# Projection halves of a hybrid block written in program order, slot by slot, with two-block attention units, unscaled queries and first values as plain products

## The chip, the cores and the metric

The kernel runs on one core of a Trainium2 chip. The metric is the device time of one execution in microseconds (us). A core has a matrix engine (PE in the profile, with its weight loads as PEld), a vector engine (DVE), a scalar engine (ACT), a general engine (POOL), and a sync engine (SP) that here only issues transfers. Each engine works through its own list of instructions in order and waits at an instruction until what it needs is there.

## The reference

One layer, one sequence of 2048 tokens, width 1024, all in float32. Cut to what matters:

```python
mod = silu(c) @ w_ada + b_ada;  shift, scale, gate = split(mod, 3)
h = rms_norm(x, norm_w) * (1 + scale) + shift
a, b, g_conv, q, k, v, g_attn, m_conv, m_attn = split(h @ w_in)     # one projection to 10240 columns
u = silu(layer_norm(depthwise_causal_conv(a * sigmoid(b)))) * silu(g_conv)   # 31 taps
y_conv = u @ w_conv_out
q, k = rope(rms_norm(q)), rope(rms_norm(k))                          # 12 heads of 128
# 3 groups of 4 heads, dilation 1, 4, 16: blocks of 128 queries against their own and the previous key block
o = softmax over the groups' log denominators, weighted sum of the 3 groups' outputs
y_attn = (o * silu(g_attn)) @ w_attn_out
y = sigmoid(m_conv) * y_conv + sigmoid(m_attn) * y_attn
x + gate * (y @ w_out)
```

## The kernel before

**The projection.** The tokens are worked in two halves of 1024. In a half the 80 column blocks of 128 are done in pairs, 40 pairs (the code's "quads": two column blocks by two token blocks of 512 by two halves of the depth). A quad is multiplied by a Strassen-Winograd scheme with seven products (`PRODUCTS`) in place of eight. Each operand is split into two float32r parts, a high one (ACT copies, `shB`, `shT`) and a low one (the difference, `slB`, `slT`, on POOL or DVE), and a product is 12 matmuls of 128x512 (hi*hi, hi*lo, lo*hi for four depth chunks). One product is a slot. The quarters of the activations and their sums are A11, A12, A22, S1 to S4; weight quarters B11 to B22 and sums T1 to T4 come from POOL in the first half of the tokens and are stored for the second (`tT_d`).

**Order of quads in a half.** First two value quads in alternating slots, then 16 query, key and value quads (`qkv_quad`; called the chain below), then 22 more: 8 for the convolution's input (`ab_quad`) and 14 gates. `quad` is a generator; a slot runs one product, copies or adds its bank to a scratch tile ("spare_hi", "spare_lo", 8 places of 512 columns) and prepares the weights of a slot four later.

**Rotary step.** `rotate` squares a query or key quad (ACT), sums the squares over the head with PE (`pssq`, `pssk`, L490), brings the sums through memory into columns (`ssq_d`, `stq`), takes the power -1/2 on POOL (L136), and brings the result through memory back as rows (`rsq`, `rsk`, L530). DVE multiplies the rotated quad by them (L534), and it is stored to `qk_d`. Values are turned by PE (`ptv`, L453) and stored.

**Attention** (`attend`) works one block of 128 queries at a time, in steps of one slot each: loads, scores on PE (`ps`, L583) with mask, scale and minimum on DVE (L592) and exponential on ACT (L593); transposes on PE (`ptp`, L598) with a copy on DVE (L600); values on PE (`po`, L620). For the last group `weigh` combines the three groups. The blocks of the last quads are worked beside the first gates of the half. The convolution's taps (`conv_parts`) are DVE instructions, 3.1 of them a slot on the average.

**What sets the order.** PE's list is the program's order (`manual_schedule`). All other lists are set by a scheduler that plans with its own time line, except where `keep` pins an instruction. Stores of the weight sums are issued by ACT, all other transfers by SP.

**After the halves** comes a tail: attention's and the convolution's output projections, and the last projection by the same seven products.

Of the kernel before, what the change touches and what calls it, by code (L numbers as in the profile page):

```python
# [38 lines left out]
WS = 5  # L39
# [18 lines left out]
def tile_hybrid_block(  # L58
# [17 lines left out]
    BANKS = {"z": 2, "s": 1, "t": 2, "o": 3}  # L76
# [7 lines left out]
    tab_d = dram.tile([2, 64, HS], F32, name="tab_d")  # L84
# [15 lines left out]
    t_d = {}  # L100
    keep = tc.keep_in_program_order
# [37 lines left out]
    edge.tile([P, 120], F32, name="edge")  # L139
# [11 lines left out]
    wraw_c = tc.tile_pool(name="wr", bufs=10, side="right", reuse_waits="tile")  # L151
# [4 lines left out]
    pe_order.__enter__()  # L156

    PLACE = {"A11": (0, 0), "A12": (1, 0), "A22": (1, 1), "S1": (0, 1), "S2": (0, 2), "S3": (1, 2), "S4": (0, 3)}
# [20 lines left out]
    rp, at, cv, gpa, xh = {}, {}, {}, {}, {}  # L179
# [11 lines left out]

    def spare_tiles():
        spares[:] = [quarter_tile(1, 3, hl, f"spare_{hl}", F32) for hl in ("hi", "lo")]
# [13 lines left out]

    conv_todo = []
# [4 lines left out]

    def column_steps(half, c0, c1, lo_engines):

        q, got = {}, []
        where = {"B11": (0, c0), "B21": (1, c0), "B12": (0, c1), "B22": (1, c1)}

        def load(name):
            t = q[name] = wr.tile([P, 4, P], F32, tag="wr", name=f"w{name}_{half}_{c0}")  # L220
            src = w_in[where[name][1] // P, where[name][0]] if name in where else t_d[name, c0]
            nc.sync.dma_start(t.rearrange("p k c -> p (k c)"), src)

        def combine(name, dst, x0, x1):
            if dst is None:
                dst = wr.tile([P, 4, P], F32, tag="wr", name=f"w{name}_{c0}")
# [3 lines left out]
        def split(name, eng):  # L230
# [4 lines left out]
            if half == 0 and name not in where:  # L235
                t_d[name, c0] = dram.tile([P, 512], F32, name=f"t{name}_{c0}_d")
                nc.scalar.dma_start(t_d[name, c0], q[name].rearrange("p k c -> p (k c)"))

        def fetch(n):
            if half:  # L240
# [6 lines left out]
        def step(n):  # L247
            if half == 0:
                if n == 2:
                    combine("T1", q["B11"], q["B12"], q["B11"])  # L250
                    combine("T2", None, q["B22"], q["T1"])
                if n == 4:
                    combine("T3", q["B12"], q["B22"], q["B12"])
                if n == 6:
                    combine("T4", q["B21"], q["B21"], q["T2"])
            split(PRODUCTS[n][1], nc.vector if n in lo_engines else nc.gpsimd)

        return got, step, fetch, load

    def quad(name, got, sink, place=None, cut=lambda x: x, side="s"):  # L260
# [4 lines left out]
        def product(n, ps, more=False):  # L265
            ah, al = quarters[PRODUCTS[n][0]]
            wh, wl = got.pop(0)
            terms = [t for k in range(4) for t in ((wh[:, k], ah[:, k]), (wh[:, k], al[:, k]), (wl[:, k], ah[:, k]))]
            for m, (w, x) in enumerate(terms):
                nc.tensor.matmul(ps, w, x, start=(m == 0 and ps.name not in first), stop=(m == 11 and not more),  # L270
                                 skip_group_check=True)
            first.add(ps.name)

        def kept(ps, t, col):
            dst = place(t, col) if place else scratch()
            nc.scalar.activation(dst, cut(ps), AF.Copy)  # L276
            return dst

        product(0, pa, True)
        s1 = kept(pa, 0, 0)  # L280
        yield
        pb = bank(side, f"pb{name}")
        product(1, pb)
        nc.vector.tensor_tensor(s1, s1, cut(pb), op=ALU.add)
        sink(0, 0, s1)
        yield
        product(2, pa, True)
        s2 = kept(pa, 0, 1)
        yield
        pc = bank(side, f"pc{name}")  # L290
        product(3, pc, True)
        s5 = kept(pc, 1, 0)
# [1293 lines left out]
```

## Time and profile before

| | |
|---|---|
| median of 3 runs | 2673.28 us (2673.21 to 2675.82) |
| profiled execution | 2674.34 us, span from first to last instruction 2672.6 us |
| busy share of the span | PE 89%, DVE 69%, ACT 44%, POOL 49% |
| granted PE clock, mean | 0.943 |
| transfers | 462.80 MB, 173 GB/s over the span |

The time lies 1.7 us above the span. A busy PE is not a fast PE: a matmul that runs at half the clock is busy twice as long, so the number of matmuls in a stretch says more than the busy share. In the trace a row's duration of a matmul overlaps the next one's, so starts are compared.

### The profile page before, as it was taken

What the parts mean: (1) busy time and instruction counts of PE and PEld (TensorE: products, weight loads), DVE (VectorE), ACT (ScalarE), POOL (GpSimd) and SP (SyncE); (2) the same over time, 40 slices, a digit from 0 to 9 for tenths busy, and PEclk for the clock granted to TensorE, in tenths of its full rate; (3) what the DMA queues carried; (4) which work ended last, traced back from release to release, by engine and by line L of the source; (5) the groups of instructions that cost most, each with busy time, mean ns of one, the idle gap of its engine ahead of it and who ended that gap; (6) DMA issues with size and microseconds to landing.
All of it is one profiled execution on the core that took longest, in us unless ns stands there. A gap on an engine that the chain in (4) does not pass through costs nothing. (4 is left out here: it accounts for less than half of the span.)

```text
span 2672.6 us, 36779 instructions
## 1 busy us (share of the span) xinstructions
PE 2390.2 (89%) x11580; PEld 1940.7 (73%) x11580; DVE 1842.7 (69%) x3034; ACT 1184.5 (44%) x2313; POOL 1300.8 (49%) x1014
## 2 busy tenths in 40 slices
PE   6766788988888999999888899888999998999999
PEld 5545666777667888877667777776788887788787
DVE  2779655555588999995755444459899985777744
ACT  3544444444745444465444444465344443332221
POOL 3567755575444677876544444333565760000131
PEclk7787889999999999999989999999999999999999
DMA  7266545565545444575455556654554559876553
GB/s 266 78 172 227 149 135 163 155 197 172 173 145 162 148 154 167 182 232 151 135 149 154 162 144 187 197 165 140 165 160 131 159 173 316 255 228 222 184 166 107
DMA packets 349708, 462.80 MB, mean 173 GB/s; under 512 B 43460, under 2 KB 176068, under 8 KB 349384
## 3 DMA queue, kind: packets, MB, share of 16 engines
q1 hardware_dynamic: 312200, 392.77, 49.3%
q10 hardware_dynamic: 37312, 67.67, 6.8%
q8 instruction: 92, 1.51, 0.2%
q14 instruction: 104, 0.85, 0.1%
HBM read 295.14 MB, written 164.63 MB: 172 GB/s over the span
## 5 line engine op out<-in xcount | busy, mean ns | idle before, releaser
L233 POOL TENSOR_TENSOR slB<-wB,shB 128x512 fp32r<-128x512 f32 x196 | 271.8, 1387 | 342.0 <-ACT shB L232 289.5
L233 POOL TENSOR_TENSOR slT<-wT,shT 128x512 fp32r<-128x512 f32 x200 | 278.5, 1393 | 213.5 <-ACT shT L232 186.8
L232 ACT ACTIVATE shB<-wB 128x512 fp32r<-128x512 f32 x240 | 150.6, 628 | 276.2 <-PE paab L270 41.3
L233 POOL TENSOR_TENSOR slT<-wB,shT 128x512 fp32r<-128x512 f32 x120 | 171.7, 1441 | 109.8 <-ACT shT L232 74.2
L232 ACT ACTIVATE shT<-wT 128x512 fp32r<-128x512 f32 x200 | 125.9, 629 | 214.3 <-issue 20.9
L600 DVE COPY pT<-ptp 128x256 f32<-128x256 f32 (+1 forms) x192 | 73.2, 382 | 175.7 <-PE ptp L598 175.0
L352 DVE SCALAR_TENSOR_TENSOR ce<-us,pair_taps,ce 128x512 f32<-128x512 f32 x240 | 180.4, 752 | 5.5
L323 DVE SCALAR_TENSOR_TENSOR ce<-ut,chan,ce 128x512 f32<-128x512 f32 x240 | 178.6, 744 | 0.0
L336 DVE SCALAR_TENSOR_TENSOR cq<-ut,chan,cq 128x512 f32<-128x512 f32 x208 | 155.0, 745 | 0.5
L227 POOL TENSOR_TENSOR wB<-wB,wB 128x512 f32<-128x512 f32 x80 | 112.8, 1410 | 54.8 <-DVE slB L233 49.8
L593 ACT ACTIVATE sm<-sm,osb 128x256 f32<-128x256 f32 (+1 forms) x128 | 59.8, 467 | 168.1 <-DVE osb L592 143.4
L598 PE MATMUL ptp<-ident,sm 128*128 128x128 f32 x332 | 74.5, 295 | 58.8 <-ACT sm L593 57.8
L620 PE MATMUL po<-v,pT 128*128 128x128 f32 x560 | 99.0, 285 | 23.1 <-DVE pT L600 20.7
L232 ACT ACTIVATE shT<-wB 128x512 fp32r<-128x512 f32 x120 | 75.3, 628 | 99.2 <-PE pbab L270 11.1
L592 DVE CUSTOM_DVE_ANT_0 sm<-ps,mask 128x256 f32<-128x256 f32 (+1 forms) x192 | 73.1, 381 | 63.0 <-PE ps L583 38.5
L620 PEld LDWEIGHTS po<-v,pT 128*128 128x128 f32 x560 | 86.3, 197 | 36.4 <-DVE pT L600 24.8
L135 POOL TENSOR_SCALAR stf<-stf 128x4 f32<-128x4 f32 x4 | 1.3, 324 | 199.6 <-DVE stf L1235 199.6
L598 PEld LDWEIGHTS ptp<-ident,sm 128*128 128x128 f32 x332 | 42.6, 148 | 72.9 <-ACT sm L593 70.1
L583 PE MATMUL ps<-qk 128*128 128x128 f32 x384 | 79.7, 292 | 0.7 <-DVE osb L622 0.7
L1407 ACT ACTIVATE yh<-yq 128x512 fp32r<-128x512 f32 x48 | 27.3, 623 | 118.2 <-POOL yq L1401 45.3
L606 POOL COPY stm<-part 128x4 f32<-128x4 f32 x64 | 13.6, 214 | 121.6 <-DMA part<-acc_d 97.9
L296 POOL TENSOR_TENSOR spare_lo<-spare_lo 128x512 f32<-128x512 f32 x41 | 66.5, 1621 | 4.4 <-ACT spare_lo L276 4.4
(789 smaller groups left out, 8175.5 us busy)
## 6 DMA issues: line engine op xcount, KB each, us to landing
wB<-in_w_in_dram SPq DMA_DIRECT2D x280, 256.0 KB
wT<-tT_d SPq DMA_DIRECT2D x160, 256.0 KB
tT_d<-wB ACTq DMA_DIRECT2D x120, 256.0 KB
qk<-qk_d SPq DMA_DIRECT2D x192, 128.0 KB
v_d<-vev SPq DMA_DIRECT2D x48, 256.0 KB
qk_d<-spare_hi SPq DMA_DIRECT2D x48, 256.0 KB
qk_d<-spare_lo SPq DMA_DIRECT2D x48, 256.0 KB
v<-v_d SPq DMA_DIRECT2D x192, 64.0 KB
```

The costliest lines, as they stand in the source:

```text
L227: nc.gpsimd.tensor_tensor(dst, x0, x1, op=ALU.subtract)
L232: nc.scalar.activation(h, q[name], AF.Copy)
L233: eng.tensor_tensor(l, q[name], h.bitcast(F32), op=ALU.subtract)
L296: nc.gpsimd.tensor_tensor(s3, s3, s5, op=ALU.add)
L323: stt(box["e"], e[:, 1 + j : 513 + j], chan[:, cb, 2 * j : 2 * j + 1], box["e"], op0=ALU.mult, op1=ALU.add)
L336: stt(box["o"], o[:, 2 + j : 514 + j], w, psum_o, op0=ALU.mult, op1=ALU.add)
L352: stt(dst, box["both"][:, 1 + j : 513 + j], pair_taps[:, cb, j : j + 1], box["e"], op0=ALU.mult, op1=ALU.subtract if j == 0 else ALU.add)
L583: nc.tensor.matmul(ps[:, P * i : P * i + P], box["q"], kt, start=True, stop=True)
L592: nc.vector.tensor_tensor_reduce(sm[:, :w], ps[:, :w], m[:, 256 - w :], ISQ, 3e38, ALU.add, ALU.min, low)
L598: nc.tensor.transpose(pt[:, P * i : P * i + P], box["sm"][:, P * i : P * i + P], ident)
L600: nc.vector.tensor_copy(pT[:, :w], pt[:, :w])
L620: nc.tensor.matmul(po[:, :P], box["pT"][:, P * i : P * i + P], vt, start=(i == 0), stop=(i == nk - 1))
```

## The change

All five engines' lists are now the program's order during the value, query and key quads of a half, and up to 6 slots after the last of them; outside of it the scheduler orders the other engines as before. A slot runs in a fixed sequence of named places.

```diff
-    LEAD = WS - 1
-        next(running[i], None)
-        prepare(s + LEAD)
-        for f in agenda.pop(s, ()):
-            f()
-        if waiting and (s % 4 != 3 or i % half_jobs >= QJ):
-            main.enter(attend(*waiting.pop(0)))
-        for f in main.turn():
-            f()
+        if waiting and s % 2:
+            for d, where, f in unit(*waiting.pop(0)):
+                at_slot(s + 3 + d, f, where)
+        run_agenda(s, "load")
+        ask(s + AHEAD + 2)
+        for where in ("act", "pe", "vec"):
+            run_agenda(s, where)
+        prepare(s + AHEAD)
+        run_agenda(s, "act2")
+        next(running[i], None)
+        run_agenda(s, "tail")
+        run_agenda(s, "store")
-WS = 5
+WS, WR, AHEAD = 4, 10, 3
+MANUAL, ORDER_END = (True, True), 6
-    BANKS = {"z": 2, "s": 1, "t": 2, "o": 3}
+    BANKS = {"z": 2, "s": 2, "t": 1, "u": 1, "o": 2}
```

Attention goes by units of two blocks (up to 128x512 scores in a bank), a new one every second slot, and each step has its place. Queries are stored unscaled; the root of a query's squares is turned by PE into a column (`queries`, `query_roots`) and multiplies the scores in the instruction that adds the mask. Keys are scaled as before, at fixed slots.

```diff
-            nc.vector.tensor_tensor_reduce(sm[:, :w], ps[:, :w], m[:, 256 - w :], ISQ, 3e38, ALU.add, ALU.min, low)
+            rq = heads_rq[half, u - u % 2]
+            for i, b in enumerate(bs):
+                a, z = cols[i][0], 256 * i + 256
+                nc.vector.tensor_tensor_reduce(sm[:, a:z], ps[:, a:z], m[:, 256 - (z - a) :], rq[:, b, u % 2 : u % 2 + 1], 3e38,
+                                               ALU.add, ALU.min, box["low"][i])
-        return (load, fetch, scores, turn_p, values, *((turn_o,) if g == 0 else ()))
+        return ((-3, "load", load), ((-1, "store", fetch) if half else (-2, "load", fetch)), (0, "pe", scores), (1, "act", exps), (2, "tail", turn_p), (3, "act", weigh),
+                (3, "tail", values), (4, "store", keep), (5, "pe", turn_o), (6, "store", keep_o))
...
-        squares(0)
-        for d, f in ((1, lambda: sums(0)), (1, lambda: squares(1)), (2, lambda: sums(1)), (2, part(0, 0)), (3, roots), (3, part(0, 1)),
-                     (4, part(1, 0)), (5, part(1, 1)), (5, spread), (7, lambda: scaled(0)), (8, lambda: scaled(1))):
-            at_slot(s0 + d, f)
+            sq = ((e4 + 1, 0, 0), (e5, 1, 1), (e5 + 1, 0, 1), (e6 + 1, 1, 0))
+            start, last = e5 + 2, e6 + 3
...
+        at_slot(last, rows, "act2")
+        if which == 0:
+            at_slot(last + 1, queries, "tail")
+            at_slot(last + 2, query_roots)
+        else:
+            at_slot(last, keys, "store")
+            at_slot(last + 1, key_roots)
+            at_slot(last + 2, key_spread, "store")
+            s = last + 3
+            for i in range(2):
+                at_slot(s + i, key_scale(i))
+                at_slot(s + i + 1, store(i), "load")
```

In the chain, the first product of a quad now stands between the fifth and the sixth product of the quad before it. The first two value quads of the first half are plain products, 16 of them (`PLAIN`), that need only A11 and A21 for their first six slots; two low parts in three or more of the seven go to DVE in the first half (`QKV_LO`), and the sums of two banks that POOL added are now added by DVE from the bank. The tanh gates come first in a half, three of them before the convolution's first quad, and the silu gates last. Weight sums are stored by SP a slot after they are made. Rotary tables are stored already permuted for each group and loaded anew when the group changes. Attention in the first half may begin only when the second half's activations are prepared (`later_done`, slot 78).

```diff
+        for i in range(len(chain)):
+            j = len(jobs) + i
+            slots += [(j, n) for n in range(early, 5)] + [(j + 1, 0)] * (i + 1 < len(chain)) + [(j, 5), (j, 6)]
+            early = True
+    PLAIN = ((0, "B11", "A11", "C11"), (1, "B11", "A11", "C11"), (0, "B12", "A11", "C12"), (1, "B12", "A11", "C12"),
+             (0, "B11", "A21", "C21"), (0, "B12", "A21", "C22"),
...
+QKV_LO = (((1, 3, 5), (1, 3, 5), (0, 1, 3, 5, 6)), ((), (), (1, 3, 5)))
+FIRST_GATES, BETWEEN = 3, ((1, 1, 1, 1, 2, 1, 2, 2), (1, 1, 2, 1, 1, 1, 1, 3))
-        gates = [(GC0, g_d, AF.Silu), (MC0, mc_d, AF.Tanh), (MA0, ma_d, AF.Tanh)]
+        todo = [(gate_quad, half, g, cb) for g in ((MC0, mc_d, AF.Tanh), (MA0, ma_d, AF.Tanh), (GC0, g_d, AF.Silu)) for cb in range(0, KC, 2)]
-                nc.scalar.dma_start(t_d[name, c0], q[name].rearrange("p k c -> p (k c)"))
+                at_slot(slot_now[0] + 1, lambda: nc.sync.dma_start(d, t), "store")
```

**ACT, start of the kernel, before.** `xsq` are the squares of the second token block, on which A12, A22 and all sums S wait; `shT` are high parts of weight sums.

```order
L237 DMA tT_6656_d<-wB_0_6656_213 128x512
L237 DMA tT_6912_d<-wB_0_6912_215 128x512
L232 ACTIVATE shT_0_6656_398<-wT_6656_396 128x512
L237 DMA tT_6656_d<-wT_6656_396 128x512
L237 DMA tT_6656_d<-wB_0_6656_365 128x512
L232 ACTIVATE shT_0_6912_421<-wT_6912_419 128x512
L237 DMA tT_6912_d<-wT_6912_419 128x512
L702 ACTIVATE xsq_1_428<-hf_1_172 128x512
```

The same place after:

```order
L289 ACTIVATE shB_p_1_381<-wB_p_222 128x512
L289 ACTIVATE shB_p_2_385<-wB_p_224 128x512
L289 ACTIVATE shB_p_3_400<-wB_p_226 128x512
L289 ACTIVATE shB_p_4_417<-wB_p_220 128x512
L883 ACTIVATE xsq_1_435<-hf_1_179 128x512
```

The squares stood behind high parts of POOL's weight sums; they now stand behind high parts of loaded weights, and no sum is needed there.

**ACT, first gates of the first half, before.** `L402` is a gate's function, `L593` the exponential of a block's scores; a table load stands wherever the function's set changes.

```order
L402 ACT_TABLE_LOAD
L402 ACTIVATE spare_hi<-spare_hi 128x512
L593 ACT_TABLE_LOAD
L593 ACTIVATE sm_0_4_5808,stm_0_4_5807<-sm_0_4_5808,stm_0_4_5807 128x256
L608 ACTIVATE stm_0_4_5807<-stm_0_4_5807 128x3
L403 DMA g_d<-spare_hi 128x512
L232 ACTIVATE shT_0_2304_5889<-wB_0_2304_5597 128x512
L613 ACTIVATE part_0_4_5755<-part_0_4_5755,stm_0_4_5807 128x128
L402 ACT_TABLE_LOAD
```

After, the only load in the gates of this half stands where the silu gates begin, behind the last tanh gate:

```order
L451 ACTIVATE spare_hi<-spare_hi 128x512
L452 DMA ma_d<-spare_hi 128x512 x2
L246 ACTIVATE shT_0_2048_8133<-wB_0_2048_7984 128x512
L327 ACTIVATE spare_lo<-pag_g_d_0_8113 128x512
L246 ACTIVATE shB_0_2048_8167<-wB_0_2048_7986 128x512
L451 ACT_TABLE_LOAD
```

ACT's whole list holds 48 table loads before and 6 after.

**DVE, chain, scaling of a quad, before (a query quad of the first half).** `sm` is the instruction on a block's scores, `pT` the copy of its transposes.

```order
L600 COPY pT_0_2_4325<-ptp_0_2_4323 128x128
L503 SCALAR_TENSOR_TENSOR tmk_4_10_4506<-spare_lo,hw,cos_665 128x512
L504 SCALAR_TENSOR_TENSOR tmk_4_11_4507<-spare_lo,hw,sin_666 128x512
L534 TENSOR_TENSOR spare_hi<-spare_hi,rsq_4_4238 128x1024 x2
L592 ISA sm_0_3_4378,osb_0_3_4377<-ps_0_3_4375,mask_120 128x128
```

After (a key quad of the second half):

```order
L778 ISA sm_1_2_13572,osb_1_2_13571<-ps_1_2_13566,mask_120,rqq_3_12414 128x256
L778 ISA osb_1_2_13571 128x1
L644 TENSOR_TENSOR spare_lo<-spare_lo,rsk_4_13561 128x1024
L512 TENSOR_TENSOR spare_hi<-spare_hi,pcv_4_13453 128x512
L796 COPY pT_1_0_13598<-ptp_1_0_13593 128x512
L644 TENSOR_TENSOR spare_lo<-spare_lo,rsk_4_13561 128x1024
```

The scaling of queries is gone from DVE's list. That of keys stands in two parts, one in each of two slots, with a bank's addition and a unit's copy behind the first.

More of the change, by code (lines that the diff above doesn't have):

```diff
@@ L262, in quad, with step @@
         pa = bank("z", f"pa{name}")
         first = set()
[L265 to L271, printed above, removed]
+        def step(n, ps, more=False):
+            product(PRODUCTS[n][0], ps, got.pop(0), ps.name not in first, not more)
@@ L302, in quad @@
         yield
-        product(6, pa)
-        if place:
-            kept(pa, 1, 0)
+        step(6, pa)
         sink(1, 0, pa, s1)
@@ L445, in qkv_quad, with step, evict @@
-        return quad(n, got, sink, place, cut, side)
-    def turn_v(half, _, u0, g, reg, n):
-        s0 = slot_now[0]
+        cut, place = token_views(g)
+        at = slots_of[half, which, pair]
+        (turn_v if which == 2 else rotate)(half, which, u0, g, reg, n, at)
+        pa = bank("z", f"pa{n}")
+        first = set()
+        def step(m, ps, more=False):
+            product(PRODUCTS[m][0], ps, got.pop(0), ps.name not in first, not more)
+            first.add(ps.name)
+        def evict(dst, ps):
+            nc.scalar.activation(dst, cut(ps), AF.Copy)
@@ L1032, in attention_shut @@
     def attention_shut():
-        assert not waiting and not main.parts
         shut(at)
@@ L1161, in tile_hybrid_block @@
                 load_ai0(n - 3)
[L1162 removed]
+    run_conv(len(conv_todo))
+    assert not agenda, agenda
     shut(gpa)
```

1044 lines of the change are left out of this document (628 added, 416 removed), and 3 rows, old and new, of the table PLAIN.

## Prediction

> **What bounds the kernel now.** I read the page first, then the busy time by stages, then PE's waits in the stages that lose most, and last the rows around single waits. On the page, PE is the busiest engine, and nothing else comes near it:
>
> ```profile
> span 2672.6 us, 36779 instructions
> PE 2390.2 (89%) x11580; PEld 1940.7 (73%) x11580; DVE 1842.7 (69%) x3034; ACT 1184.5 (44%) x2313; POOL 1300.8 (49%) x1014
> ```
>
> The stages: the start with the first two value quads (to 136), the chain of the first half (to 658), its first gates with attention beside them (to 850), gates with the convolution, then the same for the second half (value quads from 1168, chain from 1214, gates from 1709), and the tail from 2213. In each row stand the limits, the length, the busy time and count of each engine, the granted clock and the transfers.
>
> ```profile
> core 0: us, PE busy (x) PEld busy (x) DVE busy (x) ACT busy (x) POOL busy (x), PEclk, DMA share, GB/s
> 0.00:136.00 136.00, 94.04 (x449) 73.49 (x450) 65.85 (x80) 56.88 (x90) 65.86 (x65) 0.79 0.50 175
> 136.00:658.00 522.00, 422.98 (x2203) 336.42 (x2203) 324.36 (x434) 233.71 (x503) 340.21 (x222) 0.89 0.58 170
> 658.00:850.00 192.00, 157.13 (x798) 128.88 (x797) 138.01 (x407) 114.14 (x248) 76.45 (x91) 0.94 0.50 155
> 850.00:1150.00 300.00, 300.00 (x1325) 248.39 (x1324) 281.56 (x402) 135.61 (x234) 232.24 (x185) 1.00 0.50 170
> 1168.00:1214.00 46.00, 39.94 (x169) 32.79 (x169) 30.64 (x40) 25.00 (x37) 28.91 (x21) 0.93 0.71 216
> 1214.00:1709.00 495.00, 436.64 (x2446) 356.40 (x2445) 266.67 (x391) 225.63 (x478) 233.21 (x154) 0.94 0.54 154
> 1709.00:1950.00 241.00, 217.20 (x1072) 179.27 (x1072) 188.05 (x475) 136.75 (x288) 96.15 (x103) 0.96 0.57 171
> 2213.00:2672.00 459.00, 442.51 (x1904) 355.35 (x1902) 292.76 (x449) 128.72 (x215) 50.60 (x40) 0.98 0.66 209
> ```
>
> From 850 to 1150 PE is never idle and has the full clock: 300 us for 1325 matmuls, 0.2264 us each; I take 0.2252, since a few of them are other work. That gives the floor of any stage, if I know how many of its matmuls are products (line 270) and how many are small:
>
> ```profile
> 136.00:658.00 522.00, 364.88 (x1345) 267.49 (x1345) 0.89 0.58 170
> 658.00:850.00 192.00, 117.75 (x446) 86.20 (x447) 0.94 0.50 155
> 1214.00:1709.00 495.00, 351.42 (x1346) 259.35 (x1346) 0.94 0.54 154
> 1709.00:1950.00 241.00, 177.24 (x699) 134.70 (x700) 0.96 0.57 171
> ```
>
> Small ones, and a wait with what it does to the clock, on PE's list (start, duration, matmul, and the idle time before it):
>
> ```profile
> 406.28 0.79 PE L270 MATMUL paq<-S_hi,shT 128*128 128x512 f32 x1 [2.04 <-ACT spare_lo L276]
> 406.87 0.63 PE L270 MATMUL paq<-S_lo,shT 128*128 128x512 f32 x1
> ...
> 409.43 0.51 PE L270 MATMUL paq<-S_lo,shT 128*128 128x512 f32 x1
> ...
> 421.54 0.61 PE L620 MATMUL po<-v,pT 128*128 128x128 f32 x4
> ...
> 422.46 0.47 PE L270 MATMUL paq<-A_hi,shT 128*128 128x512 f32 x1
> 428.62 0.64 PE L490 MATMUL pssq<-sqq,sel 128*32 128x128 f32 x16
> 429.19 0.71 PE L620 MATMUL po<-v,pT 128*128 128x128 f32 x4
> ```
>
> From 421.54 to 422.46 PE ran nine small matmuls, 0.1 us each; the 16 for the sums of squares took 0.57, 0.036 each, and a half has 384 of these. So the floor of the first chain is 1345 x 0.2252 = 303, plus 384 x 0.036 = 14, plus 474 x 0.1 = 47: 364. It takes 522: 158 too much, of which 99 are idle and the rest slow matmuls. In the same way: first gates 446 x 0.2252 + 352 x 0.1 = 136 of 192, 56 too much; second chain 303 + 14 + 72 = 389 of 495, 106 too much (58 idle); its gates 157 + 37 = 195 of 241, 46 too much. The rest of the gates and the tail have little to lose.
>
> Slow matmuls come from waits: after the 2.04 us of waiting above, the next matmuls start 0.427 apart (six gaps in 406.87 to 409.43), in place of 0.23. A wait of 2 us costs some 3.5. [...]
>
> What PE waits for, in 100 to 300, 300 to 650, 650 to 850 and 1300 to 1690 (total us, times, longest):
>
> ```profile
> PE ptv L453 <- ACT vev L455: 17.9, 3, 10.1
> ...
> PE ptp L598 <- ACT sm L593: 22.0, 13, 5.2
> PE po L620 <- DVE pT L600: 15.6, 9, 4.9
> ...
> PE pta L639 <- DVE osb L622: 8.6, 4, 3.6
> PE ps L583 <- DVE osb L622: 8.1, 6, 2.2
> PE ptp L598 <- ACT sm L593: 7.7, 8, 2.5
> ...
> PE ptp L598 <- ACT sm L593: 23.9, 11, 4.3
> PE po L620 <- DVE pT L600: 19.3, 7, 3.9
> ```
>
> No throughput stands behind these: DVE and ACT have 324 and 234 us of work in 522. PE meets a transpose whose exponential, or values whose copy, stands late in another engine's list.
>
> **The change part by part.**
>
> *Start, -26.* Before, PE waits twice in the first 100 us:
>
> ```profile
> 49.55 13.81 PE L704 MATMUL xm<-ones,xsq 128*128 128x1 f32 x64 [9.86 <-ACT xsq L702]
> 93.00 0.80 PE L270 MATMUL pav<-S_hi,shT 128*128 128x512 f32 x1 [8.66 <-ACT S_hi L750]
> ```
>
> The squares stand behind weight sums, the product at 93.00 waits for the sums S. Plain products need neither until their seventh slot. That takes away 9.9 + 8.7, and behind each wait I allow 18 slow matmuls at 0.2 us more, as behind 406.28: 7.2. Together 26, so the chain starts at about 110. Bounds: 0 if loads are what is late, and 35 if the values' turn (17.9 in the waits) goes as well.
>
> *Chains, -102 and -51.* The first product of the next quad covers the turn of a quad; a unit's exponentials come one slot after its scores, transposes at the end of the second slot, values one later. A slot has 12 x 0.2252 = 2.7 us of products, so the two waits above (37.6 and 43.2 us in the two stretches, with their slow matmuls) have covers of 2.7 us and more, and I let them go. Scaling of queries goes from DVE: 24 instructions in all, as the rows with `rsq` below show. POOL loses 53 low parts in the first chain to DVE, which needs 816 ns for what takes POOL 1387.
>
> ```profile
> L233 POOL TENSOR_TENSOR slB<-wB,shB 128x512 fp32r<-128x512 f32 x196 | 271.8, 1387 | 342.0 <-ACT shB L232 289.5
> L233 DVE TENSOR_TENSOR slB<-wB,shB 128x512 fp32r<-128x512 f32 x44 | 35.9, 816 | 4.7 <-ACT shB L232 4.5
> L534 DVE TENSOR_TENSOR spare_hi<-spare_hi,rsq 128x1024 f32<-128x1024 f32 x16 | 26.6, 1700 | 15.1 <-DMA rsq<-rsq_d 15.1
> L534 DVE TENSOR_TENSOR spare_lo<-spare_lo,rsq 128x1024 f32<-128x1024 f32 x8 | 9.4, 1218 | 12.7 <-DMA rsq<-rsq_d 12.7
> ```
>
> DVE then has about 324 + 53 x 0.816 - 18 = 349 us of work in the first chain, below the 448 that I give that chain; POOL 340 - 74 = 266. What is late next is the keys' root. Its way through memory, in the chain of the second half:
>
> ```profile
> 1562.39 2.01 SPq L517 DMA_DIRECT2D ssq_d<-ssrq  x3
> ...
> 1577.93 3.43 DVE L534 TENSOR_TENSOR spare_hi<-spare_hi,rsq 128x1024 f32<-128x1024 f32 x2 [3.02 <-DMA rsq<-rsq_d]
> ```
>
> 15.5 us from the first store to the multiplication. After, three slots lie between, 12 us at 4.0 a slot, so DVE waits about 4 us for each of the six key quads of a half, with the bank's addition and the unit's copy behind it, and PE behind these: 6 x 4 = 24. Before, five slots of 4.7 lay between, and even so DVE waited 27.8 us in all for the roots of queries (the two rows with `rsq` above). For the remaining waits between engines I keep 0.28 us a slot, 31 over 112 slots: that is about a tenth of a product's time; the nearest row is the stage from 850 to 1150, where they are 0, and the far one the chain now, 1.4 a slot. Together 55 in place of 158 and 106: -102 (to whole us) and -51, ends 20 and 110 for each.
>
> *First gates, -23 and -26.* The tanh gates come first, tanh and exponential no longer alternate:
>
> ```profile
> L402 ACT ACT_TABLE_LOAD x23 | 29.5, 1283 | 0.4
> L593 ACT ACT_TABLE_LOAD x22 | 28.2, 1283 | 4.7 <-ACT spare_lo L402 3.1 <-ACT spare_hi L402 1.2
> ```
>
> Some 42 loads go, 54 us of ACT's time, nearly all in these two stretches; ACT is at 114 of 192 there, so most of it costs nothing by itself, and what counts is the exponentials' delay and the waits listed for 650 to 850. Units also halve the count of small DVE and ACT instructions there. The three waits listed for 650 to 850 make 24.4 us; I let 23 go in the first half. There 17 blocks more than before come into the gates; PE's work for them leaves the chain, at no net price. In the second half only 9 of 48 units are left for the gates, so of its 46 more goes, 26. Ends: nothing gained, or all but 20 and 10.
>
> *Value quads of the second half*, 46 us against a floor of 168 x 0.2252 = 38: -4.
>
> *Added:* two more slots of products, 24 x 0.2252 = 5.4, and 24 turns of roots at 0.1: +8. The tail keeps its instructions: 0, covered by its own PE list. DVE's additions of banks in place of POOL's lie beside products, in the 349 above with room of 99; without that room each of them delays the bank's next user by as long as it takes.
>
> Sum: -26 - 102 - 23 - 4 - 51 - 26 + 8 = -224. The profiled execution took 2674.34, so 2450; the median of the runs, 2673.28, is 1 lower, which I neglect.
>
> **Rivals.**
>
> *Nearly free of stalls.* If memory answers in 12 us when SP's list is shorter, the chains keep 20 each (-70) and the gates 20 less in all: 2360. For it speaks the stage from 850, which has none; against it the 15.5 us.
>
> *Waits become shorter, but the slow matmuls stay.* If short idle times of the chain, in every slot, keep the clock low, the chains win only from their idle shares, 99 of 158 and 58 of 106. With the kept 55 scaled the same way, the chains then give some 92 in place of 153: 2511. [...]
>
> *Half the gain.* If PE's waits pass on to others (`ps` on its bank, which is freed by DVE; loads of SP behind stores in program order), half of the 206 outside of the start remains: -26 - 103 + 8 = -121, so 2553. DVE's 349 us of 448, in fixed order, and uneven slots speak for it.
>
> *Slower.* One mechanism: every engine's list is in order, so a slot lasts as long as its longest one; a DVE slot with half of a key's scaling (1.7, as a query's above), two low parts (1.6) and a bank's addition is over 4 us, and PE waits for the unit's copy behind them. It decides where it costs more than 1.0 us on each of the 224 chain slots, since 224 x 1.0 eats the gain; a slot is then 5.0, above the 4.66 (522 / 112) of now. With 1.2 us: 2719. Against it: DVE's mean is 349 / 112 = 3.1 a slot, and a light slot follows a heavy one.
>
> *No change:* if loads and not order set the chains. The DMA share is 0.58 at 170 GB/s there, against 0.66 at 209 in the tail: little speaks for it.
>
> **How the numbers follow.** Forecast 0.40, nearly free of stalls 0.18, slow matmuls 0.12, half 0.20, slower 0.08, no change 0.02. The range takes in the second to the fourth: 2345 (chains 20, gates 20 and 10, start -35: -102 more) to 2560. Under it and over it lie the edges of these cases and the last two, 2 in 10. Faster by over 0.2%, about what a measurement tells from no change, 0.91; within 0.01; slower 0.08.
>
> **What will show it.** Right, if: the first chain begins at about 110; a chain takes about 448; the granted clock there is 0.96 or more; PE's waits for exponentials and copies fall to a few us; DVE waits 3 to 5 us for `rsk` twelve times and never for `rsq`; ACT has 6 table loads; the gates from 850 on and the tail keep their lengths. Wrong, if chain slots stay above 4.5 us: then the wait that took the old one's place stands on top of PE's list, and I expect it on DVE's instruction on scores or on SP's loads. Faster than forecast, if no `rsk` wait reaches PE.

## The result and the profile after

The changed kernel takes 2516.81 us (median of 4 runs, 2515.44 to 2520.3), the kernel before 2674.55 us beside it: ratio 0.941 (0.940 to 0.943). The forecast was 2450, its range 2345 to 2560: faster, as forecast, and within the range, but 158 us gained in place of 224.

The page, in the same two lines as before:

```profile
span 2515.7 us, 34990 instructions
PE 2347.1 (93%) x11628; PEld 1903.8 (76%) x11628; DVE 1763.4 (70%) x2889; ACT 1072.5 (43%) x2163; POOL 1100.2 (44%) x860
```

PE is idle for 169 us in place of 282. The stages after, with the same columns as before: start, first chain, two parts of the first half's gates, value quads and chain of the second half, and its first gates.

```profile
0.00:120.00 120.00, 98.73 (x488) 75.72 (x489) 72.97 (x93) 60.79 (x96) 38.41 (x40) 0.84 0.61 204
120.00:573.00 453.00, 399.20 (x2112) 311.61 (x2111) 303.58 (x425) 198.88 (x403) 231.26 (x157) 0.94 0.61 183
573.00:850.00 277.00, 263.08 (x1351) 220.78 (x1350) 211.97 (x482) 138.87 (x350) 149.20 (x137) 0.98 0.59 188
850.00:1070.00 220.00, 214.02 (x942) 176.26 (x941) 212.66 (x299) 104.44 (x183) 177.40 (x137) 1.00 0.54 184
1070.00:1124.00 54.00, 45.61 (x177) 36.16 (x178) 32.91 (x45) 20.82 (x31) 14.16 (x11) 0.85 0.46 147
1124.00:1596.00 472.00, 435.37 (x2560) 354.45 (x2561) 244.09 (x443) 205.66 (x456) 176.69 (x129) 0.97 0.56 167
1596.00:1850.00 254.00, 247.15 (x1210) 206.92 (x1209) 191.66 (x368) 120.18 (x269) 128.62 (x110) 0.99 0.58 185
```

The boundaries of stages are the starts of the first product of the first query quad, first gate, first value quad of the second half and so on, on PE's list. By them the 156.9 us between the spans are:

| stage | before | after | forecast | measured |
|---|---|---|---|---|
| start and first value quads | 135.8 | 120.0 | -26 | -15.8 |
| first chain | 522.2 | 453.3 | -102 | -68.9 |
| gates, first half | 516.2 | 496.5 | -23 | -19.7 |
| value quads, second half | 40.2 | 54.5 | -4 | +14.3 |
| second chain | 494.4 | 471.3 | -51 | -23.1 |
| gates, second half | 507.8 | 463.5 | -26 | -44.3 |
| tail | 456.0 | 456.6 | 0 | +0.6 |

The forecast's +8 for added work lies in these stages. By the prediction's own floor (products 0.2252 us, its estimate, where those of before start 0.227 apart from 850 to 1150; small ones 0.1, sums of squares 0.036) the chains' excess fell from 158 to 98 and from 106 to 72. The counts are in the rows above and in these two of the products alone:

```profile
120.00:573.00 453.00, 346.36 (x1344) 257.32 (x1344) 0.94 0.61 183
1124.00:1596.00 472.00, 336.11 (x1346) 246.40 (x1347) 0.97 0.56 167
```

First chain: 303 + 14 + 384 x 0.1 = 355 of 453. Second: 303 + 14 + 830 x 0.1 = 400 of 472. Of the 98, 54 are idle (453.0 - 399.2), of the 72, 37. Attention's work has moved between stages too: the first chain has 90 small matmuls fewer than before (384 for 474), the second 114 more (830 for 716), some 9 and 11 us at 0.1 each.

Most of the first chain's 69 us were gained in its first five quads, where little or no attention runs: they took 187 us before and take 136 now.

```profile
136.00:323.00 187.00, 128.68 (x620) 99.48 (x620) 144.22 (x125) 84.11 (x138) 129.57 (x74) 0.83 0.62 182
120.00:256.00 136.00, 115.35 (x566) 86.05 (x565) 101.71 (x100) 61.25 (x106) 88.19 (x59) 0.91 0.61 169
```

PE's waits in the two chains (total us, times, longest). The waits for exponentials, 22.0 and 23.9 us in the prediction's list, are gone; others stand in their place:

```profile
PE ptv L570 <- ACT vev L572: 10.9, 4, 6.0
PE pcq L314 <- DVE spare_hi L512: 9.3, 2, 9.0
PE po L819 <- DVE pT L796: 7.5, 3, 4.8
PE pak L314 <- ACT spare_lo L510: 7.1, 2, 5.1
PE pcv L314 <- DVE spare_hi L512: 4.9, 1, 4.9
...
PE po L819 <- DVE pT L796: 28.3, 4, 10.5
```

The first chain waits for banks and values, a little each; the second has one main cause, copies of transposes (the last row), four times and 28 of 37 us. The reason for the third of these stands ahead of them on the list, the keys' scaling on DVE:

```profile
1397.34 2.70 SPq L628 DMA_DIRECT2D ssk_d<-ssrk  x4
...
1403.34 2.93 POOL L138 TENSOR_TENSOR stk<-stk,mhalf 128x16 f32<-128x16 f32 x1
1406.27 1.13 SPq L217 DMA_DIRECT2D cos<-tab_d  x2
1407.45 1.23 SPq L217 DMA_DIRECT2D sin<-tab_d  x2
1408.78 0.53 SPq L638 DMA_DIRECT2D rsk_d<-stk  x1
1414.30 1.08 SPq L641 DMA_DIRECT2D rsk<-rsk_d  x2
...
1419.57 1.22 DVE L644 TENSOR_TENSOR spare_hi<-spare_hi,rsk 128x1024 f32<-128x1024 f32 x1 [13.52 <-DMA rsk<-rsk_d]
1420.71 0.68 DVE L796 COPY pT<-ptp 128x512 f32<-128x512 f32 x1
...
1421.44 0.80 PE L819 MATMUL po<-pkv,pT 128*128 128x128 f32 x2 [9.28 <-DVE pT L796]
```

22 us from the first of these stores to the multiplication. The power is done at 1406.3; the roots' store leaves at 1408.78, behind four table loads; the load that reads them back leaves 5.5 us after the store, and DVE has its values 5 us after that. DVE waits 13.5 us, the unit's copy stands directly behind, and PE waits 9.3 for that copy.

This is the longest of the twelve key quads. Over all of them the way takes 17.9 us on the average (15.0 to 22.2), of which 1.4 to 5.5 lie between the roots' store and the load back. In nine of the twelve the roots' store follows the power within 0.1 us, so work ahead of it on SP's list is not the rule. Over the whole run DVE waits like this for 91.7 us, 7.6 for each key quad:

```profile
L644 DVE TENSOR_TENSOR spare_lo<-spare_lo,rsk 128x1024 f32<-128x1024 f32 x16 | 20.8, 1302 | 58.8 <-DMA rsk<-rsk_d 58.8
L644 DVE TENSOR_TENSOR spare_hi<-spare_hi,rsk 128x1024 f32<-128x1024 f32 x8 | 9.9, 1235 | 32.9 <-DMA rsk<-rsk_d 32.9
```

### The profile page after: what moved, and what is told of

Same layout as the page of the kernel before. It is cut to its first block, busy times and chain, and to the rows that moved or that the text cites. A ratio compares the mean times of both kernels' runs of the same rounds, so it can differ in the third digit from the quotient of the medians.

```text
span 2515.7 us, 34990 instructions
## 1 busy us (share of the span) xinstructions
PE 2347.1 (93%) x11628; PEld 1903.8 (76%) x11628; DVE 1763.4 (70%) x2889; ACT 1072.5 (43%) x2163; POOL 1100.2 (44%) x860
## 5 line engine op out<-in xcount | busy, mean ns | idle before, releaser
L247 POOL TENSOR_TENSOR slT<-wT,shT 128x512 fp32r<-128x512 f32 x192 | 259.6, 1354 | 283.7 <-ACT shT L246 253.4
L247 POOL TENSOR_TENSOR slB<-wB,shB 128x512 fp32r<-128x512 f32 x142 | 190.5, 1342 | 194.5 <-ACT shB L246 172.1
L247 POOL TENSOR_TENSOR slT<-wB,shT 128x512 fp32r<-128x512 f32 x94 | 126.8, 1353 | 174.7 <-ACT shT L246 148.9
L778 DVE CUSTOM_DVE_ANT_0 sm<-ps,mask,rqq 128x256 f32<-128x256 f32 (+1 forms) x192 | 78.1, 444 | 102.5 <-PE ps L766 73.8
L796 DVE COPY pT<-ptp 128x512 f32<-128x512 f32 (+2 forms) x96 | 58.8, 612 | 55.2 <-PE ptp L794 54.9
L247 DVE TENSOR_TENSOR slB<-wB,shB 128x512 fp32r<-128x512 f32 x92 | 70.8, 771 | 37.8 <-ACT shB L246 19.0
L819 PE MATMUL po<-v,pT 128*128 128x128 f32 x560 | 84.8, 283 | 11.7 <-DVE pT L796 11.7
L819 PEld LDWEIGHTS po<-v,pT 128*128 128x128 f32 x560 | 77.1, 196 | 19.5 <-DVE pT L796 12.2
L766 PEld LDWEIGHTS ps<-qk 128*128 128x128 f32 x512 | 69.8, 201 | 0.3 <-issue 0.2
L825 ACT ACTIVATE osb<-po 128x256 f32<-128x256 f32 x64 | 24.7, 386 | 87.9 <-PE po L819 87.3
L644 DVE TENSOR_TENSOR spare_lo<-spare_lo,rsk 128x1024 f32<-128x1024 f32 x16 | 20.8, 1302 | 58.8 <-DMA rsk<-rsk_d 58.8
```

The costliest lines, as they stand in the source:

```text
L247: eng.tensor_tensor(l, q[name], h.bitcast(F32), op=ALU.subtract)
L766: nc.tensor.matmul(ps[:, c : c + P], box["q"][i], kt, start=True, stop=True)
L778: nc.vector.tensor_tensor_reduce(sm[:, a:z], ps[:, a:z], m[:, 256 - (z - a) :], rq[:, b, u % 2 : u % 2 + 1], 3e38, ALU.add, ALU.min, box[" ...
L819: nc.tensor.matmul(po[:, P * i : P * i + P], box["pT"][:, c : c + P], vt, start=(m == 0), stop=(m == count[i] - 1))
```

## The experiments

All were timed against the kernel before on the same chip, which took 2678, 2671 and 2673 us in the three groups of runs, so the ratios are what compares across groups. The stages are those of one profiled execution of each, the times are medians.

| run | median us | ratio (95%) | start | chain 1 | gates 1 | values | chain 2 | gates 2 |
|---|---|---|---|---|---|---|---|---|
| before | 2674.55 | 1 | 135.8 | 522.2 | 516.2 | 40.2 | 494.4 | 507.8 |
| after | 2516.81 | 0.941 (0.940 to 0.943) | 120.0 | 453.3 | 496.5 | 54.5 | 471.3 | 463.5 |
| e1_no_root_wait | 2480.85 | 0.927 (0.924 to 0.930) | 122.0 | 441.0 | 495.2 | 54.5 | 451.1 | 462.4 |
| e2_order_off | 2503.80 | 0.935 (0.932 to 0.938) | 136.4 | 443.4 | 502.3 | 43.7 | 452.6 | 466.3 |
| e2b_order_first | 2495.65 | 0.932 (0.929 to 0.935) | 120.7 | 452.9 | 496.5 | 44.4 | 450.1 | 466.0 |
| e3_silu_first | 2527.50 | 0.945 (0.942 to 0.947) | 123.7 | 455.7 | 500.9 | 54.1 | 472.5 | 465.9 |
| e8_short_cover_off | 2491.65 | 0.932 (0.930 to 0.934) | 135.1 | 440.5 | 507.5 | 44.0 | 443.9 | 464.4 |
| e7_no_early_off | 2535.21 | 0.949 (0.947 to 0.951) | 137.7 | 458.5 | 489.9 | 45.0 | 486.9 | 457.6 |
| e10_queries_scaled_off | 2558.81 | 0.958 (0.955 to 0.960) | 136.0 | 472.4 | 501.0 | 45.0 | 483.5 | 466.5 |
| e13_three_undone_off | 2556.24 | 0.958 (0.955 to 0.960) | 135.2 | 473.2 | 496.1 | 43.3 | 492.0 | 458.2 |
| e9_order_start | 2501.04 | 0.937 (0.935 to 0.938) | 120.9 | 457.2 | 499.4 | 44.0 | 454.8 | 466.0 |
| b1_before_tanh_first | 2634.90 | 0.986 (0.984 to 0.989) | 138.1 | 522.6 | 493.9 | 41.0 | 494.7 | 494.0 |
| e11_first_short | 2483.11 | 0.930 (0.928 to 0.932) | 122.4 | 452.5 | 501.9 | 43.8 | 442.5 | 463.5 |
| e12_first_short_x_pool | 2503.16 | 0.938 (0.935 to 0.940) | 124.4 | 471.0 | 500.4 | 43.3 | 448.3 | 467.5 |

**The keys' roots.** The multiplication keeps its place and size but reads nothing late:

```diff
         def key_scale(i):
-            return lambda: tt(reg[i], reg[i], box["rs"], op=ALU.mult)
+            return lambda: tt(reg[i], reg[i], reg[i], op=ALU.mult)
```

> Keys are multiplied by themselves in place of by their roots, so that DVE doesn't wait for the roots' landing; every transfer and instruction stays, and the values are not the reference's. Theory A (the keys' roots are the term that was sized too small): DVE's 92 us of waits for rsk go, with them PE's 28 us of waits for pT in the second chain, some 10 in the first and the slow matmuls behind them: first chain 453 to about 438, second 472 to about 438, together 2470 us. Theory B (something else in the fixed order is late directly behind): PE waits at the next place, 2505 us or more.

36 us less: theory A, if not all of its 46. The group's wait is 0, the second chain gets 20 us shorter and the first 12; PE's waits for pT in 1130 to 1570 fall from 28.3 to 6.6 us, the second row below.

```profile
L644 DVE TENSOR_TENSOR spare_lo<-spare_lo 128x1024 f32<-128x1024 f32 x16 | 22.1, 1381 | 0.0
...
PE po L819 <- DVE pT L796: 6.6, 3, 3.4
```

So 92 us of DVE's waiting cost the kernel 32 in the chains. The first chain keeps 441 - 355 = 86 us of excess, the second 51, that don't come from DVE's waits for roots.

**Program order.** Two runs let the scheduler order DVE, ACT, POOL and SP, in both halves or in the second alone; PE's list stays by hand in both:

```diff
-MANUAL, ORDER_END = (True, True), 6
+MANUAL, ORDER_END = (False, False), 6     # e2_order_off; (True, False) in e2b_order_first
```

> The four engines beside PE are ordered by the scheduler in both halves, as in the kernel before; everything else is as after. Theory A (program order carries the chains' gain of 92 us, the other parts little): about 2600 us, with PE's waits for exponentials and copies back at 20 us a chain. Rival (two-block units, unscaled queries and the next quad's early product carry it, the order little): 2500 to 2540 us; it may even be faster, since a scheduler can put other work into the waits for roots.

> Program order in the first half's chain only, scheduler in the second. The second chain gained 22 us in all, the value quads ahead of it lost 14. Theory A (order carries the gain): second chain about 490, value quads about 44: 2525 us. Rival (order costs the second half the waits for roots and the taps in the value quads): second chain 450, value quads 42, together about 2482 us.

The rivals were right. Without program order on four engines the kernel takes 2504 us: the intervals of the two ratios lie apart, so the fixed order costs some 13 us (16 by the ratios). Theory A falls: order is not what shortened the chains. By stages the fixed order gives 16 us at the start and 9 in the gates, and takes back 10 in the first chain, 11 in the second half's value quads, and 19 in the second chain. With order in the first half alone the second chain takes 450 us and the value quads 44, as the rival said; the whole, 2496, can't be told from that with the scheduler in both (0.932 and 0.935, whose intervals overlap). With the scheduler in both DVE still waits 64 us for roots, but PE's waits for pT in 1130 to 1570 are 12.2 us:

```profile
PE po L819 <- DVE pT L796: 12.2, 4, 5.7
```

Of the 14 us that the second half's value quads lost, the scheduler gives back 11. One place is seen in the trace of after, where 16 of the convolution's last taps stand nearly in a row on DVE's fixed list, ahead of a bank's addition for which PE waits 6.2 us:

```profile
1080.65 10.26 DVE L401 SCALAR_TENSOR_TENSOR ce<-us,pair_taps,ce 128x512 f32<-128x512 f32 x13
...
1094.26 1.01 DVE L512 TENSOR_TENSOR spare_hi<-spare_hi,pbv 128x512 f32<-128x512 f32 x1
1095.42 0.76 PE L314 MATMUL pcv<-S_hi,shT 128*128 128x512 f32 x1 [6.22 <-DVE spare_hi L512]
```

**Order at the start alone**, to keep its 16 us:

```diff
+    at_slot(slots_of[0, Q, 0][0], order_shut, "enter")
```

> Program order only from the start of the kernel to the first slot of the first chain, the scheduler everywhere else. By the stages of the runs so far: the start as with program order (121 in place of 136), the rest as in e2_order_off: 2504 - 15 = 2489 us. Rival (the shorter start only moves the wait into the first chain, which took 453 behind a start of 121 and 443 behind one of 136): 2498 us or more.

The rival, 2501: the start takes 121, but the first chain behind it 457 in place of 443. The end of the first chain comes at 578 us, at 580 with the scheduler everywhere, and at 573 with program order in both. So an earlier start is mostly given back there. What is late at the chain's beginning, in the trace of after, is first a place for a turned value, held until an earlier one is stored:

```profile
153.45 0.60 ACT L572 ACTIVATE vev<-ptv 128x512 f32<-128x512 f32 x1 [12.69 <-DMA v_d<-vev]
154.98 1.05 ACT L510 ACTIVATE spare_hi<-paq 128x512 f32<-128x512 f32 x1
156.06 1.06 DVE L512 TENSOR_TENSOR spare_hi<-spare_hi,pcq 128x512 f32<-128x512 f32 x1 [0.72 <-ACT spare_hi L510]
157.17 0.79 PE L314 MATMUL pcq<-S_hi,shB 128*128 128x512 f32 x1 [9.02 <-DVE spare_hi L512]
```

ACT waits 12.7 us for a store to land, the eviction behind it is late, DVE's addition and PE follow. A fourth place was not tried.

**What carries the chains.** Three parts were undone with the scheduler on, each against e2_order_off. First the distance between a unit's steps on PE's list:

```diff
-(2, "tail", turn_p), (3, "act", weigh), (3, "tail", values)
+(1, "tail", turn_p), (2, "act", weigh), (2, "tail", values)
```

> As e2_order_off (2504 us), but a unit's transposes stand one slot after its scores and its values two, as in the kernel before, in place of two and three. Theory (the places of attention's steps on PE's list carry most of the chains' gain): PE's waits for exponentials and copies come back, 40 us in each chain with the slow matmuls behind them: chains about 480 and 490, 2575 us. Rival (halving the count of small instructions carries it): under 2520 us.

The theory falls: no loss, if anything a gain (0.932 against 0.935, with intervals that overlap). The second chain takes 444 us; the wait for pT there is 2.6 us in place of 12.2.

```profile
PE po L819 <- DVE pT L796: 2.6, 2, 2.0
```

So the longer distance, to which the forecast gave the waits for exponentials and copies, is not what removed them, with the scheduler on. The early product:

```diff
-            slots += [(j, n) for n in range(early, 5)] + [(j + 1, 0)] * (i + 1 < len(chain)) + [(j, 5), (j, 6)]
+            slots += [(j, n) for n in range(7)]
```

> As e2_order_off (2504 us), but the first product of a quad stands behind the last of the quad before it, as in the kernel before. Theory (the early product covers the turn of a quad): 15 turns in a chain cost 1.5 to 2 us each again, 2550 us. Rival (the turn was covered already, since most quads change without a wait in the trace of before): within 8 us of 2504.

31 us more (36 by the ratios), below the theory's 46 and far above the rival: the chains lose 15 and 34 us, the gates win back 12 and 9. What returns are PE's waits for the additions of banks on DVE, 25 us in 1130 to 1570, where e2_order_off has 0.4. The two largest:

```profile
PE pcq L314 <- DVE spare_hi L512: 8.6, 4, 2.5
PE pck L314 <- DVE spare_lo L512: 8.0, 4, 2.9
```

The queries' scaling:

```diff
-        else:
+        if True:            # roots of queries through memory too, as those of keys
             at_slot(last, keys, "store")
             ...
                 at_slot(s + i, key_scale(i))
```

> As e2_order_off (2504 us), but queries are scaled on DVE by roots that come through memory as keys' roots do, at the keys' slots, and besides have their roots in the scores' instruction, so they are scaled twice and the values are not the reference's. Theory (unscaled queries took waits out of the chains): twelve more waits for roots of about 2.7 us (64 us for twelve key quads in the run with the scheduler is 5 each) and 24 more instructions of 1.3 us on DVE, of which PE sees half: 2535 us. Rival (hidden): within 8 us of 2504.

55 us more (60 by the ratios), over the theory's 31, the largest of the three: the chains lose 29 and 31 us. The run is not a plain return to the kernel before: queries wait three slots for their roots where they had five, the turn of the roots on PE and the power for it stay, and the rotary instructions of some queries are packed into fewer slots. So the 55 us may be more than what unscaled queries saved. DVE's waits for the queries' roots add 37.5 us to those for keys, and PE's waits for pT in 1130 to 1570 grow from 12.2 to 24.5 us:

```profile
L644 DVE TENSOR_TENSOR spare_hi<-spare_hi,rsq 128x1024 f32<-128x1024 f32 x16 | 26.3, 1684 | 27.6 <-DMA rsq<-rsq_d 27.6
L644 DVE TENSOR_TENSOR spare_lo<-spare_lo,rsq 128x1024 f32<-128x1024 f32 x8 | 12.0, 1537 | 9.9 <-DMA rsq<-rsq_d 9.9
...
PE po L817 <- DVE pT L794: 24.5, 9, 5.8
```

A scaled query also keeps its scratch places until it is scaled and stored. PE's longest wait in the chains of the kernel before is of this kind: an eviction on ACT waits for such a query's store, and PE for the eviction.

```profile
238.22 1.04 ACT L276 ACTIVATE spare_hi<-paq 128x512 f32<-128x512 f32 x1 [10.55 <-DMA qk_d<-spare_hi]
239.31 0.79 PE L270 MATMUL paq<-S_hi,shT 128*128 128x512 f32 x1 [14.06 <-ACT spare_hi L276]
```

All three edits together:

> The scheduler orders, and three parts are undone together: no early product, transposes and values a slot earlier, queries scaled too (their values then wrong). If the parts add up: 2504 + 33 + 57 - 10 = 2584 us, and the remaining 90 us to the kernel before belong to the two-block units, the gates' order and the value quads. If they cover the same waits: under 2565 us. If each shelters the others: 2610 us or more.

2556 us, no more than with scaled queries alone: the parts don't add up (31 + 55 - 12 over 2504 would be 2578). That they cover the same waits was the reading set down for such a result; no run took two of them away at a time. The second chain is then at 492 us, where it was before (494), with 11 us more of attention's work in it; the first at 473, 49 shorter than before. Of these 49, 34 lie in the first five quads (153 us for 187 before, 136 after), so attention's two-block units can't explain them; some 9 are attention's work that left for the gates. The rest was not split further: the plain value quads ahead of it, low parts and banks' additions on DVE, and a later start of attention are all in it.

**The order of the gates**, undone in the kernel after, and done alone in the kernel before:

```diff
-((MC0, mc_d, AF.Tanh), (MA0, ma_d, AF.Tanh), (GC0, g_d, AF.Silu))     # after
+((GC0, g_d, AF.Silu), (MC0, mc_d, AF.Tanh), (MA0, ma_d, AF.Tanh))     # e3_silu_first; b1 makes the reverse edit in the kernel before
```

> The silu gates come first in a half again, as before, so that silu and exponential alternate. Theory (table loads delay exponentials in the gates): some 35 to 45 loads of 1.28 us return, the gates beside attention lose about 15 us in the first half and 5 in the second: 2537 us. Rival (ACT is at half load there, so loads are hidden, and the gates gained by the units alone): within 5 us of 2517.

> The kernel before with one edit: tanh gates first in a half, silu gates last. Theory (the new order of gates is worth what its reversal cost after, 10 us, or more, since all of attention's blocks were single): 2674 - 10 to 25 = about 2657 us, 40 table loads fewer. Rival (hidden by ACT's 44%): within 5 us of the kernel before.

After, undoing costs 11 us, about half of what the theory said, and not clear of noise (0.945 against 0.941, whose intervals overlap at the edge); 4 and 2 us of it lie in the gates. In the kernel before, the edit gives about 37 us, more than expected: its gates get 22 and 14 us shorter, with four table loads left beside exponentials and gates in place of 45.

```profile
L593 ACT ACT_TABLE_LOAD x2 | 2.6, 1283 | 0.0
L402 ACT ACT_TABLE_LOAD x2 | 2.6, 1283 | 0.0
```

In the trace of after, tanh gates and exponentials follow each other in turn with 27 changes between 584 and 805 us, and no load stands from 387.5 to 897.7; in that of before a load stands at each of the 42 changes between silu gates and exponentials (668 to 850 and 1719 to 1885). So the pair that no longer alternates is silu and exponential, not tanh and exponential as the prediction has it. ACT was at 114 of 192 us in the gates of before; the loads were paid all the same. That each can stand between a block's scores and its transposes is the likely reason, which no run separated.

**What the runs point to:** program order in the first half, the short distance of steps.

> Program order in the first half only and attention's transposes and values a slot earlier. If the two gains add up (8 us of each run): about 2485 us, the shortest so far; rival (an exponential that is late in the fixed order of the first chain): 2495 us or more, with the first chain above 455.

2483 us, 0.930, as expected and 34 us under the change: the shortest of the runs that leave nothing of the computation out. Its interval overlaps those of e2b_order_first and e8_short_cover_off, so that the two gains add up isn't shown. The same with the second half's activations prepared on POOL, in place of DVE:

```diff
-        nc.vector.tensor_tensor(*q, op=op)
+        nc.gpsimd.tensor_tensor(*q, op=op)     # and the multiplication by the roots, likewise
```

> As e11_first_short, with the preparation of the second half's activations (28 instructions of 0.7 to 1.8 us in the first chain) on POOL in place of DVE. Theory (PE's waits at 314 and 371 us for a bank's addition come from these instructions ahead of it on DVE): those waits go, first chain 8 to 10 us shorter, 2476 us. Rival (low parts on POOL become late instead): no change or longer.

The rival, and worse: 20 us more by the medians; of the 26 between the two profiled executions 18.5 lie in the first chain. PE's waits for DVE's additions of banks were not taken away (8.0 us for `pcv` where it was 4.9), and those for squares of queries rose from 3.9 to 10.6 us:

```profile
PE pssq L602 <- ACT sqq L589: 10.6, 5, 3.1
...
PE pcv L314 <- DVE spare_hi L512: 8.0, 1, 8.0
```

## Why the prediction was right, and where its steps failed

Direction and range held, since the frame did: a floor for each stage from counts of matmuls, and a tail that holds nothing to gain. The range is wide, 215 us for four cases. The sum misses by 67 us, and several terms are right or wrong for other reasons than given: start, chains and value quads fell short by 10, 61 and 18 us, and the second half's gates gave 18 more than forecast, which is luck.

**The term that was mis-sized** is the chains' 0.28 us a slot for the remaining waits, 31 us in each. With the roots' wait taken away, 86 and 51 us remain, 0.77 and 0.46 a slot. I took it from near the stage that has no waits, but the chains have banks, turned values and squares that PE needs within a slot or two. The fixed list is not the reason: with the scheduler 443 - 355 = 88 and 453 - 400 = 53 us stay, waits for roots included. Which waits make up this rest no run separates. These 55 and 20 us over the 31 are larger than the whole miss. (The prediction also speaks of a chain of 448 us, which is not its own sum of 420 and 444.)

**The keys' roots** were put at 4 us of DVE's waiting each, 24 us of PE's for a chain. DVE waits 7.6: the way through memory takes 17.9 us on the average, where I took 15.5 from one row, and DVE stands at the multiplication 10.2 us behind the first store, not 12. But PE pays 12 and 20 us, not 24 and 24. The mechanism was right, at the place named in the list of what would show it; DVE's wait was undersized, the share that PE sees oversized.

**The step that failed as a reason** is the one that let the waits for exponentials and copies go because of the longer distance of a unit's steps. Those for exponentials went (the ones for copies rose in the second chain, 28.3 us for 19.3), but e8_short_cover_off does without the distance and is not slower. Unscaled queries, which I priced as 18 us of DVE's time beside other work, thus at nothing, are worth up to 55 us with the scheduler, and the early product 31; taken away together they cost 52. And the waits on which I built the chains' gain were read from 300 us on, while 51 of the first chain's 69 us were gained in the five quads before 323, where PE had waited for evictions, turned values and additions of banks.

**The start** got 15.8 us of 26. Its 18 slow matmuls behind each wait were an allowance: behind 406.28 eight matmuls started at the halved clock. I gave the gain to the plain products; with the scheduler they are still there, and the first chain starts at 136.4, as before. Without the order they gave nothing, and the first chain took most of it back. Whether the order would do it without plain products no run shows.

**Gates.** In the first half 19.7 us were gained of a forecast 23, with some 9 us of attention's work added from the chain. The loads' order alone gives 22 in the kernel before, but undoing it after costs 4 there: the size was right, and how much of it is the order's stays open. In the second half 44 of a forecast 26; the order of gates alone gives 14 in the kernel before, some 11 are attention's work that moved into the second chain, and the remaining 19 were not split.

**The value quads** of the second half got 14 us longer, not 4 shorter. By the starts of products they took 40.2 us before, 2 over their floor of 38, so the 4 were not there to gain. I read the change in the chain and not what the fixed order does to the taps left over from the half before.

**Rivals.** The case nearest in time was 2511, of slow matmuls that stay. Its price for the two chains, 92 us, is what they gave (68.9 + 23.1), but by luck: the granted clock rose from 0.89 to 0.94 and from 0.94 to 0.97, so slow matmuls did not stay, while more idle time stayed than it said (54 and 37 us; its sum leaves 34 and 30). The slower rival, a fixed order in which a late instruction holds up what stands behind it, did occur, at 13 us for the whole kernel and not at 1.0 us on each slot.

**The signs.** The chain began at 120 us, not 110; the chains took 453 and 471, not 448; the clock was 0.94 and 0.97 against 0.96 or more; DVE waited 2.2 to 13.5 us for `rsk`, not 3 to 5. No wait for `rsq`, six table loads and a tail of the same length came as forecast.

## What to carry to other kernels

Fix an engine's order where its inputs are sure to be there; ahead of an instruction that waits for memory, leave it to a scheduler, or put what others wait for in front of it: 92 us of one engine's waiting reached the bound one as 32. Price a removed round trip through memory by what stands behind its wait and not by the instruction's own time. And test the parts of a large change one at a time with the rest in place, and together too, since here three parts did not add up and a part of the change that gave it its name cost time.

## What was not expected of the hardware

The same DVE instruction took 1.78 us beside a two-operand instruction on POOL and 0.74 us, less than half of that, without one. In the first chain of after:

```profile
357.79 1.74 POOL L241 TENSOR_TENSOR wB<-wB,wT 128x512 f32<-128x512 f32 x1
358.30 1.78 DVE L660 SCALAR_TENSOR_TENSOR tmq<-spare_lo,hw,cos 128x512 f32<-128x512 f32 x1
360.00 0.74 DVE L660 SCALAR_TENSOR_TENSOR tmq<-spare_lo,hw,sin 128x512 f32<-128x512 f32 x1
```

1.78 us with POOL at work for two thirds of it, 0.74 us after it is done. Over the whole run this line's 48 instructions with no two-operand instruction on POOL beside them take 0.73 to 0.75 us, and the 36 that have one beside them for over half of their time 1.42 us on the average, 1.86 at most. Why, no trace shows. The longer time beside POOL may be a reason why moving 32 instructions from DVE to POOL made the chain longer, where they took 33 us on DVE in the trace of after and 45 us on POOL in e12_first_short_x_pool. No run separated that.

A value's way through memory, store and dependent load, took 1.4 to 5.5 us from the store's issue to the load's in the twelve key quads, and 4.6 to 5.6 more to the multiplication. In the slowest (1408.78, 1414.30, 1419.57 above) the issuing queue sent nothing for nearly 5 us, since the load waited for the store, the longest of 12 such waits on that queue (32.4 us in all).

PE's clock fell in steps. In the traces of before and after the granted clock is 1 or 0.5, in 100 and 54 stretches that all, but for the last of each trace, last a whole number of 3.41 us. Behind the 2.04 us of waiting that the prediction reads it was 0.5 from 406.25 to 409.66, one step; in the step before, at clock 1, PE had been busy for 0.92 of 3.41 us. With products 0.427 us apart in that step, and 0.227 at the full clock, it cost some 1.6 us, an estimate from these numbers.
